# A fixed TensorE order for the first group of a state-space mixer

## The chip, the cores and the metric

The kernel runs on one core of one Trainium2 chip. The metric is the device time in microseconds (us) of one execution; the median of three runs before the change is 1351.42 us. TensorE (PE in the profile) multiplies, PEld is its loading of weights, VectorE is DVE, ScalarE is ACT, GpSimd is POOL, and SyncE (SP) starts most DMA transfers.

## The reference

The computation is a decoder trunk of two layers on 512 tokens of width 1024, in float32: a Mamba-2 mixer, a convolutional feed-forward block, differential attention, and a second feed-forward block. The change is in the mixer alone. Cut to what matters:

```python
zxbcdt = rms_norm(x, ln_g) @ in_w            # z | x, B, C | dt
xbc = silu(causal_dwconv(xbc, conv_w, conv_b))
dt = softplus(dt + dt_bias);  a = dt * (-exp(a_log))
# four groups of eight heads, four chunks of 128 tokens:
cb        = einsum('bclgn,bcsgn->bcgls', cc, bc)
y_diag    = einsum('bcgls,bgrcls,bcsgrp->bclgrp', cb, exp(segsum(a)), x*dt)
states    = einsum('bclgn,bgrcl,bclgrp->bcgrpn', bc, exp(a_cs[-1] - a_cs), x*dt)
# states are carried from chunk to chunk: S = S * exp(total of a) + states
y_off     = einsum('bclgn,bcgrpn,bgrcl->bclgrp', cc, states_in, exp(a_cs))
y = (y_diag + y_off + x * d_skip) * silu(z)
x = x + (rms_norm(y, per group) * norm_g) @ out_w
```

## The kernel before

A product of two float32 matrices is made of three passes in a reduced type: each operand is split into a high and a low part, and `mm3` (L196 to L198) multiplies high by high, low by high and high by low. One `mm3` on a block of 128 weight columns and 512 tokens is three matmuls; I call it a triple. A block of in_w has eight triples, one per 128 rows. Every chunk of weights is loaded by SP into a raw tile, its high part is made by ACT (`high`, L147), its low part by DVE (`low`, L151). `chunk(key)` hands out the next chunk and prepares the one two places further on in a fixed list, so asking for z's third block of group 0 prepares the first block of group 1.

The mixer is a loop over four groups. In each, `conv_block` makes B (bT), C (cT) and four blocks of x (xs): eight triples, then a convolution of three DVE steps and a SiLU on ACT. Then come four blocks of z, multiplied by the same input, with the scan of the group's four chunks between them. For chunk 0 to 3, called a, b, c and d in the code, the scan's steps are these:

- `fetch`: POOL starts the load of a row of sums, broadcast to all partitions, into m (128 x 8 x 128), and for chunks 1 to 3 of er. Tiles m have four buffers, er two.
- `decays`: POOL masks m (`affine_select`, L632), ACT takes eight exponentials (L637).
- `turned`: TensorE transposes B's chunk, ACT copies it (bt, L665).
- `masked`: TensorE multiplies C by B (cb, two instructions, L643), DVE multiplies m by it (L644).
- `tokens`: four transposes of xs (L652), then DVE makes xd (L654) and xe (L657).
- `states`: TensorE multiplies xe by bt (st, L682); for chunk 0 ACT copies the result to S (L685), for the others DVE scales the old S (L687) and adds (L688).
- `preceding`: for chunks 1 to 3, the previous S times C (yo, L673), then DVE multiplies er by it (L675).
- `products`: sixteen small matmuls xd by m (y, L696). `outputs`: DVE adds y, the skip term and er to xs (L705, L708).

ACT holds one table of functions at a time; the profile shows a load of a table (ACT_TABLE_LOAD) where SiLU and exponentials follow each other.

What sets the order: a planner simulates the program and gives each engine a list of instructions, by readiness in its own simulation and by place in the program. The engines then work through their lists in order, and an instruction whose input is late holds those behind it. `manual_schedule` for TensorE keeps the block's TensorE instructions in the order of the program. `issue_after(i)` queues what its block adds on i's engine behind i, without a wait for i to end.

Groups 1 to 3 use `woven` (L767): TensorE's order is fixed, and a table `at` says after which of z's 32 triples (`z_steps`, L731, counted from 0) which steps of the scan follow. In group 1 the table is read five triples later. Group 0 uses `weave` (L470) on `scan` (L750) and `z_blocks` (L722), and the planner orders TensorE too. In all groups the decays of chunks 0 and 1 stand in the program ahead of the third and fourth x block. The accumulator banks of the scan's steps come from a pool of four.

Of the kernel before, what the change touches and what calls it, by code (L numbers as in the profile page):

```python
# [18 lines left out]
P = 128  # L19
T = 512  # L20
D = 1024
KB = D // P
NT = T // P
# [16 lines left out]
def trunk_kernel(ctx: ExitStack, tc, x, ssm_ln_g, ssm_in_w, ssm_conv_w, ssm_conv_b, ssm_dt_bias,  # L40
# [4 lines left out]
    act, dve, pool, pe, sync = nc.scalar, nc.vector, nc.gpsimd, nc.tensor, nc.sync  # L45
# [192 lines left out]
    with tc.tile_pool(name="ph0", bufs=1) as p0:  # L238
# [24 lines left out]
        ps = aux_bank("pst")  # L263
# [117 lines left out]
        ps = aux_bank("pst")  # L381
# [134 lines left out]
    with tc.tile_pool(name="ssm_y", bufs=1) as yp, tc.tile_pool(name="ssm", bufs=1) as sp:  # L516
        def in_block(key):
            wh, wl = chunk(key)
            if key in ("in32", "in36"):
                return ps_b0 if key == "in32" else ps_b1  # L520
            ps = mm_bank("ps_" + key)
            for k in range(KB):
                state["last"] = mm3(ps, wh[:, k, :], wl[:, k, :], xgh[k], xgl[k], k == 0, k == KB - 1)
            return ps
# [16 lines left out]
        rr = [bp.tile([P, T], F32, tag="nr", name="nr_x")]  # L541
# [4 lines left out]
        ps = aux_bank("ps_dtt")  # L546
        with tc.issue_after(b1_end.ins):
            for c in range(NT):
# [12 lines left out]
                          in1=dtb.unsqueeze(1).to_broadcast([P, NT, NH]), op=ALU.add)  # L561
# [7 lines left out]
        for n in (13, 11, 9, 7, 5, 3):  # L569
# [21 lines left out]
        ncum = sp.tile([P, P], F32, name="ncum")  # L591
# [3 lines left out]
        ps = aux_bank("ps_cum")  # L595
# [10 lines left out]
        class Chunk:  # L606
# [22 lines left out]
            def decays(self):  # L629


                pool.affine_select(out=self.m, in_=self.m, pattern=[[0, HPG], [1, P]], compare_op=ALU.is_ge,  # L632
                                   fill=NEG, base=0, channel_multiplier=-1)
                for h in range(HPG):
                    v = self.m[:, 4 * (h % 2) + h // 2, :]
                    col = self.hh.start + h
                    act.activation(v, v, AF.Exp, bias=ncum[:, col:col + 1])  # L637

            def masked(self):

# [36 lines left out]
            def states(self):  # L677

                tag, c = self.tag, self.c
                if c < NT - 1:  # L680
                    ps = aux_bank("st" + tag)
                    pe.matmul(ps, self.bt, fl(self.xe), start=True, stop=True)  # L682
                    self.S = sp.tile([P, HPG, 64], F32, tag="S", name="S" + tag, bufs=2)
                    if c == 0:
                        act.activation(fl(self.S), ps, AF.Copy)  # L685
                    else:
                        dve.tensor_tensor(out=self.S, in0=self.prev.S, in1=self.per_head(et), op=ALU.mult)  # L687
                        dve.tensor_tensor(out=self.S, in0=byh(ps), in1=self.S, op=ALU.add)  # L688
# [30 lines left out]
                    add_to_stream(m, ps, 16, norm)  # L719
                    yield  # L720

        def z_blocks(g, zs):  # L722
            for b in range(4):
                ps = in_block("in%d" % (4 * g + b))
                z = sp.tile([P, T], F32, tag="z", name="z%d_%d" % (g, b), bufs=4)
                dve.tensor_tensor(out=z, in0=ps, in1=rr[0], op=ALU.mult)
                act.activation(z, z, AF.Silu)
                zs.append(z)
                yield

        def z_steps(g, zs):  # L731
            for b in range(4):
                wh, wl = chunk("in%d" % (4 * g + b))
                ps = mm_bank("ps_in%d" % (4 * g + b))
                for k in range(KB):
                    state["last"] = mm3(ps, wh[:, k, :], wl[:, k, :], xgh[k], xgl[k], k == 0, k == KB - 1)
                    if k == KB - 1:
                        z = sp.tile([P, T], F32, tag="z", name="z%d_%d" % (g, b), bufs=4)
                        dve.tensor_tensor(out=z, in0=ps, in1=rr[0], op=ALU.mult)
                        act.activation(z, z, AF.Silu)  # L740
                        zs.append(z)
                    yield

        def chunks(g, bT, cT, xs):
# [5 lines left out]
        def scan(cs):  # L750
            for t in range(NT + 1):
                if t < NT:
                    cs[t].tokens()
                    if t < NT - 1:
                        cs[t].turned()
                    cs[t].masked()
                if t == 0:
                    cs[2].decays()
                    cs[3].decays()
                if t:  # L760
                    cs[t - 1].preceding()
                    cs[t - 1].states()
                    cs[t - 1].products()
                    cs[t - 1].outputs()
                yield

        def woven(cs, g, zs):  # L767

            def pair(a, b):
                a.products()  # L770
                b.products()
                a.outputs()
                b.outputs()

            a, b, c, d = cs
            at = {0: (a.turned, b.turned, c.decays), 1: (a.masked, b.masked, d.decays),
                  10: (a.tokens,), 11: (b.tokens,), 13: (a.states,), 15: (b.preceding, b.states),
                  16: (lambda: pair(a, b), c.turned, c.masked), 18: (c.tokens,), 19: (c.preceding, d.tokens),
                  20: (d.masked,), 21: (c.states,), 24: (d.preceding,), 25: (lambda: pair(c, d),)}
            with tc.manual_schedule(engines={mybir.EngineType.PE}):  # L780
                behind = 5 if g == 1 else 0
                for n, _ in enumerate(z_steps(g, zs)):
                    for f in at.get(n - behind, ()):
                        f()

# [17 lines left out]
        for g in range(NG):  # L803
            bT = sp.tile([P, T], F32, tag="bT", name="bT%d" % g, bufs=2)
            cT = sp.tile([P, T], F32, tag="cT", name="cT%d" % g, bufs=2)
            xs_ = sp.tile([P, 4, T], F32, tag="xs", name="xs%d" % g, bufs=2)
            cs = chunks(g, bT, cT, xs_)
            for c in cs:
                c.fetch()
            conv_block(16 + g, "in%d" % (32 + g), bT)  # L810
            if g:
                prev = normed(*todo)
            conv_block(20 + g, "in%d" % (36 + g), cT)
            if g == 0:
                params_a()
            xs = [xs_[:, b, :] for b in range(4)]
            for b in range(4):
                if b >= 2:
                    cs[b - 2].decays()
                conv_block(4 * g + b, "in%d" % (16 + 4 * g + b), xs[b])  # L820
            zs = []
            if g:
                woven(cs, g, zs)
            else:
                weave(scan(cs), z_blocks(g, zs), 2, 3)
            acc = None
            for b in range(4):
                dve.tensor_tensor(out=xs[b], in0=xs[b], in1=zs[b], op=ALU.mult)
                sq = sp.tile([P, T], F32, tag="gsq", name="gsq%d_%d" % (g, b), bufs=2)
                act.activation(sq, xs[b], AF.Square)  # L830
                if b == 0:
                    acc = sq
                else:
                    a2 = sp.tile([P, T], F32, tag="gacc", name="gacc%d_%d" % (g, b), bufs=2)
                    (pool if b == 1 else dve).tensor_tensor(out=a2, in0=acc, in1=sq, op=ALU.add)
                    acc = a2
            factor = lambda: token_rsqrt(acc, sp, "g%d" % g, 512)
            if g == 0:
                params_b()
                todo = g, xs, factor()  # L840
            elif g < NG - 1:
                run(out_proj(g - 1, *prev, None))
                todo = g, xs, factor()
            else:
                op = out_proj(g - 1, *prev, None)
                for _ in range(3):
                    next(op)
                rt = factor()
                for _ in range(2):
                    next(op)  # L850
                prev = normed(g, xs, rt)
                run(op)
# [460 lines left out]
```

## Time and profile before

| | |
|---|---|
| Runs | 1350.94, 1351.42, 1352.56 us |
| Profiled execution | 1352.13 us |
| its span, first to last instruction | 1350.4 us |
| TensorE busy | 1342.4 us |
| DVE, ACT, POOL busy | 915.0, 646.2, 106.3 us |
| Group 0's x blocks, z and scan, on TensorE | from 27 to about 89 us of the span |
| Group 1's z and scan | about 122 to 158 us |
| Group 2's z and scan | about 213 to 247 us |

A row of a timeline has the start and the length in us, the engine, the line, the operation, what it writes and reads, shapes, how many in a row, and in brackets how long its engine sat idle before and what ended that. A row of stretches has the stretch and its length, then for each engine the busy us and the number of instructions, then TensorE's granted clock, the share of DMA time and GB/s. A row of waits has who waited, for whom, us in total, times, and the longest. The busy time of TensorE contains modelled ends: a matmul of 512 columns is shown as 0.39 us long while the next one starts earlier, so the distance of two starts tells more than the length.

### The profile page before, as it was taken

What the parts mean: (1) busy time and instruction counts of PE and PEld (TensorE: products, weight loads), DVE (VectorE), ACT (ScalarE), POOL (GpSimd) and SP (SyncE); (2) the same over time, 40 slices, a digit from 0 to 9 for tenths busy, and PEclk for the clock granted to TensorE, in tenths of its full rate; (3) what the DMA queues carried; (4) which work ended last, traced back from release to release, by engine and by line L of the source; (5) the groups of instructions that cost most, each with busy time, mean ns of one, the idle gap of its engine ahead of it and who ended that gap; (6) DMA issues with size and microseconds to landing.
All of it is one profiled execution on the core that took longest, in us unless ns stands there. A gap on an engine that the chain in (4) does not pass through costs nothing.

```text
span 1350.4 us, 16886 instructions
## 1 busy us (share of the span) xinstructions
PE 1342.4 (99%) x6423; PEld 1097.3 (81%) x6423; DVE 915.0 (68%) x1525; ACT 646.2 (48%) x1060; POOL 106.3 (8%) x142
## 2 busy tenths in 40 slices
PE   9999999999999999999999999999999999999998
PEld 7878788888888888888888887777888888888887
DVE  4989888788877774267754556778777773367743
ACT  5696553742444442234433556777654442134430
POOL 6230400200110000000001200000110000000000
PEclk9999999999999999999999999999999999999999
DMA  7453433432333333333323422221232332333322
GB/s 204 143 166 90 138 109 110 133 94 71 94 94 94 94 98 105 94 94 94 100 80 102 133 78 89 69 86 36 76 92 87 103 94 94 94 104 99 94 94 78
DMA packets 179825, 134.98 MB, mean 100 GB/s; under 512 B 6492, under 2 KB 163552, under 8 KB 179744
## 3 DMA queue, kind: packets, MB, share of 16 engines
q1 hardware_dynamic: 173872, 120.73, 29.7%
q0 software_dynamic: 4592, 12.08, 2.8%
q10 hardware_dynamic: 1280, 1.10, 0.2%
q8 instruction: 50, 0.82, 0.2%
q14 instruction: 31, 0.25, 0.1%
HBM read 131.64 MB, written 2.25 MB: 99 GB/s over the span
## 4 chain that ended last, share of the span: by engine, by line
PE 93%; DVE 3%; ACT 2%; issue 1%; DMA 0%; POOL 0%; SPq 0%; ACTq 0%; DVEq 0%
PE ps_g L197 6%; PE ps_g L198 6%; PE ps_g L196 6%; PE ps_u L198 6%; PE ps_u L196 6%; PE ps_u L197 6%; PE ps_in L196 4%; PE ps_in L197 4%; PE ps_in L198 4%; PE ps_d L198 3%; PE ps_d L196 3%; PE ps_d L197 3%; PE ps_d L915 3%; PE ps_d L914 3%; PE ps_d L913 3%; PE ps_o L197 2%
## 5 line engine op out<-in xcount | busy, mean ns | idle before, releaser
L196 PE MATMUL ps_u<-xgh,wh_u 128*128 128x512 f32 x352 | 137.6, 391 | 0.0
L197 PE MATMUL ps_g<-xgl,wh_g 128*128 128x512 f32 x352 | 137.2, 390 | 0.0
L196 PE MATMUL ps_g<-xgh,wh_g 128*128 128x512 f32 x352 | 137.2, 390 | 0.0
L198 PE MATMUL ps_u<-xgh,wl_u 128*128 128x512 f32 x352 | 137.2, 390 | 0.0
L198 PE MATMUL ps_g<-xgh,wl_g 128*128 128x512 f32 x352 | 137.2, 390 | 0.0
L197 PE MATMUL ps_u<-xgl,wh_u 128*128 128x512 f32 x352 | 137.1, 390 | 0.0
L196 PE MATMUL ps_in<-xgh,wh_in 128*128 128x512 f32 x304 | 126.4, 416 | 0.0
L151 DVE TENSOR_TENSOR wl_d<-wr_d,wh_d 128x1024 fp32r<-128x1024 f32 (+1 forms) x46 | 54.2, 1179 | 96.9 <-ACT wh_d L147 96.7
L197 PE MATMUL ps_in<-xgl,wh_in 128*128 128x512 f32 x304 | 119.5, 393 | 0.0
L198 PE MATMUL ps_in<-xgh,wl_in 128*128 128x512 f32 x304 | 119.4, 393 | 0.0
L147 ACT ACTIVATE wh_d<-wr_d 128x1024 fp32r<-128x1024 f32 (+1 forms) x46 | 47.1, 1024 | 130.6 <-PE ps_d L915 62.4
L874 DVE TENSOR_TENSOR uu<-ps_u,nr_f 128x512 f32<-128x512 f32 x44 | 30.4, 692 | 78.0 <-PE ps_u L198 77.9
L940 ACT ACTIVATE hh<-vg 128x512 fp32r<-128x512 f32 x44 | 27.8, 632 | 114.9 <-DVE vg L939 114.9
L197 PEld LDWEIGHTS ps_g<-xgl,wh_g 128*128 128x128 f32 x352 | 66.1, 188 | 13.9 <-DVE xgl L413 0.3
L198 PEld LDWEIGHTS ps_g<-xgh,wl_g 128*128 128x128 f32 x352 | 66.1, 188 | 13.7
L198 PEld LDWEIGHTS ps_u<-xgh,wl_u 128*128 128x128 f32 x352 | 66.1, 188 | 13.7
L197 PEld LDWEIGHTS ps_u<-xgl,wh_u 128*128 128x128 f32 x352 | 66.2, 188 | 13.6
L196 PEld LDWEIGHTS ps_g<-xgh,wh_g 128*128 128x128 f32 x352 | 66.1, 188 | 13.6
L196 PEld LDWEIGHTS ps_u<-xgh,wh_u 128*128 128x128 f32 x352 | 66.1, 188 | 13.5
L147 ACT ACTIVATE wh_g<-wr_g 128x1024 fp32r<-128x1024 f32 x44 | 46.7, 1062 | 51.6 <-PE ps_u L197 32.3
L198 PE MATMUL ps_d<-hh,wl_d 128*128 128x512 f32 x176 | 68.6, 390 | 0.0
L196 PE MATMUL ps_d<-hh,wh_d 128*128 128x512 f32 x176 | 68.6, 390 | 0.0
(359 smaller groups left out, 3180.5 us busy)
## 6 DMA issues: line engine op xcount, KB each, us to landing
wr_g<-in_ffn_up_w_dram SPq DMA_DIRECT2D x44, 512.0 KB, 3.7
wr_u<-in_ffn_up_w_dram SPq DMA_DIRECT2D x44, 512.0 KB, 3.7
wr_d<-in_ffn_down_w_dram SPq DMA_DIRECT2D x42, 512.0 KB, 3.6
wr_in<-in_ssm_in_w_dram SPq DMA_DIRECT2D x40, 512.0 KB, 3.8
m<-cumd POOLq DMA_DIRECT2D x16, 512.0 KB, 5.0
wr_out<-in_ssm_out_w_dram SPq DMA_DIRECT2D x16, 512.0 KB, 3.3
wr_k<-in_kv_w_dram SPq DMA_DIRECT2D x8, 512.0 KB, 3.7
wr_q<-in_q_w_dram SPq DMA_DIRECT2D x8, 512.0 KB, 3.6
```

The costliest lines, as they stand in the source:

```text
L147: return act.activation(self.wh[:, :self.n], self.raw[:, :self.n], AF.Copy)
L151: return eng.tensor_tensor(out=self.wl[:, :self.n], in0=self.raw[:, :self.n], in1=self.wh[:, :self.n].bitcast(F32), op=ALU.subtract)
L196: pe.matmul(ps, wh, xh, start=start, stop=False)
L197: pe.matmul(ps, wh, xl, start=False, stop=False)
L198: return pe.matmul(ps, wl, xh, start=False, stop=stop).ins
L874: dve.tensor_tensor(out=u, in0=ps, in1=r, op=ALU.mult)
L913: pe.matmul(pss[b], hh[k][:, ts], wh[:, k - k0, :], start=k == 0, stop=False)
L914: pe.matmul(pss[b], hh[k][:, ts], wl[:, k - k0, :], start=False, stop=False)
L915: pe.matmul(pss[b], hl[k][:, ts], wh[:, k - k0, :], start=False, stop=k == stop)
L940: act.activation(h, ga, AF.Copy)
```

## The change

Group 0 is woven as the others are, with a table of its own. The decays of its four chunks stand together after the eighth triple of z. The SiLU of z's second block is queued on ACT behind the last exponential of chunk 3, and what is prepared when z's third block is asked for (the high part of group 1's first block) behind the last exponential of chunk 1. The copy of the first state goes to DVE. In group 1 the states of chunks 0 and 2 come one triple later; groups 2 and 3 keep their table.

```diff
             def decays(self):
...
-                    act.activation(v, v, AF.Exp, bias=ncum[:, col:col + 1])
+                    self.decayed = act.activation(v, v, AF.Exp, bias=ncum[:, col:col + 1]).ins
...
-                    if c == 0:
+                    if c == 0 and self.g == 0:
+                        dve.tensor_copy(fl(self.S), ps)
+                    elif c == 0:
                         act.activation(fl(self.S), ps, AF.Copy)
...
-        def z_steps(g, zs):
+        def z_steps(g, zs, cs):
             for b in range(4):
-                wh, wl = chunk("in%d" % (4 * g + b))
+                if g == 0 and b == 2:
+                    with tc.issue_after(cs[1].decayed):
+                        wh, wl = chunk("in%d" % b)
+                else:
+                    wh, wl = chunk("in%d" % (4 * g + b))
...
-                        act.activation(z, z, AF.Silu)
+                        if g == 0 and b == 1:
+                            with tc.issue_after(cs[3].decayed):
+                                act.activation(z, z, AF.Silu)
+                        else:
+                            act.activation(z, z, AF.Silu)
...
             a, b, c, d = cs
-            at = {0: (a.turned, b.turned, c.decays), 1: (a.masked, b.masked, d.decays),
-                  10: (a.tokens,), 11: (b.tokens,), 13: (a.states,), 15: (b.preceding, b.states),
-                  16: (lambda: pair(a, b), c.turned, c.masked), 18: (c.tokens,), 19: (c.preceding, d.tokens),
-                  20: (d.masked,), 21: (c.states,), 24: (d.preceding,), 25: (lambda: pair(c, d),)}
+            both = lambda: pair(a, b)
+            rest = lambda: pair(c, d)
+            if g == 0:
+                at = {0: (a.turned, b.turned), 7: (a.decays, b.decays, c.decays, d.decays),
+                      11: (a.tokens,), 12: (b.tokens,), 14: (a.states,), 16: (a.masked, b.masked),
+                      17: (b.preceding, b.states), 20: (both, c.turned, c.masked), 22: (c.tokens,),
+                      23: (c.preceding, d.tokens), 24: (d.masked,), 26: (c.states,), 28: (d.preceding,),
+                      29: (rest,)}
+            else:
+                at = {0: (a.turned, b.turned, c.decays), 1: (a.masked, b.masked, d.decays),
+                      10: (a.tokens,), 11: (b.tokens,), 13: (a.states,), 15: (b.preceding, b.states),
+                      16: (both, c.turned, c.masked), 18: (c.tokens,), 19: (c.preceding, d.tokens),
+                      20: (d.masked,), 21: (c.states,), 24: (d.preceding,), 25: (rest,)}
+            if g == 1:
+                at[14], at[22] = at.pop(13), at.pop(21)
...
             for b in range(4):
-                if b >= 2:
+                if g and b >= 2:
                     cs[b - 2].decays()
...
-            if g:
-                woven(cs, g, zs)
-            else:
-                weave(scan(cs), z_blocks(g, zs), 2, 3)
+            woven(cs, g, zs)
```

More of the change, by code (lines that the diff above doesn't have):

```diff
@@ L720, in out_proj @@
                     yield
-        def z_blocks(g, zs):
+        def z_steps(g, zs, cs):
             for b in range(4):
[L724 to L729, printed above, removed]
-        def z_steps(g, zs):
-            for b in range(4):
-                wh, wl = chunk("in%d" % (4 * g + b))
+                if g == 0 and b == 2:
[3 more added lines that the diff above has]
+                    wh, wl = chunk("in%d" % (4 * g + b))
                 ps = mm_bank("ps_in%d" % (4 * g + b))
@@ L739, in z_steps @@
                         dve.tensor_tensor(out=z, in0=ps, in1=rr[0], op=ALU.mult)
-                        act.activation(z, z, AF.Silu)
+                        if g == 0 and b == 1:
[3 more added lines that the diff above has]
+                            act.activation(z, z, AF.Silu)
                         zs.append(z)
@@ L748, in chunks @@
             return cs
[L750 to L765, printed above, removed]
         def woven(cs, g, zs):
@@ L775, in woven @@
             a, b, c, d = cs
-            at = {0: (a.turned, b.turned, c.decays), 1: (a.masked, b.masked, d.decays),
-                  10: (a.tokens,), 11: (b.tokens,), 13: (a.states,), 15: (b.preceding, b.states),
-                  16: (lambda: pair(a, b), c.turned, c.masked), 18: (c.tokens,), 19: (c.preceding, d.tokens),
-                  20: (d.masked,), 21: (c.states,), 24: (d.preceding,), 25: (lambda: pair(c, d),)}
+            both = lambda: pair(a, b)
[13 more added lines that the diff above has]
+                at[14], at[22] = at.pop(13), at.pop(21)
             with tc.manual_schedule(engines={mybir.EngineType.PE}):
                 behind = 5 if g == 1 else 0
-                for n, _ in enumerate(z_steps(g, zs)):
+                for n, _ in enumerate(z_steps(g, zs, cs)):
                     for f in at.get(n - behind, ()):
```

## The prediction

> **What bounds the kernel now.** I read the page first (busy shares and the chain that ended last), then TensorE's waits, then stretches of the state-space stage, and last the engines' timelines inside them.
>
> ```profile
> span 1350.4 us, 16886 instructions
> PE 1342.4 (99%) x6423; PEld 1097.3 (81%) x6423; DVE 915.0 (68%) x1525; ACT 646.2 (48%) x1060; POOL 106.3 (8%) x142
> PE 93%; DVE 3%; ACT 2%; issue 1%; DMA 0%; POOL 0%; SPq 0%; ACTq 0%; DVEq 0%
> ```
>
> TensorE (PE) is busy for all but 8.0 us of 1350.4 and is 93% of the chain. Every us of TensorE's own sequence counts, and nothing else counts unless TensorE waits for it. Its total waits are few:
>
> ```profile
> PE warm L262 <- DVE ones L202: 1.1, 1, 1.1
> PE st L682 <- DVE xe L657: 0.8, 2, 0.6
> ```
>
> The first is the start of the program. The second is group 1's two state matmuls, which the last part of the change touches. But "busy" hides delays, because a matmul's end is modelled: it lasts 0.39 us, while the next starts earlier. So I count starts. Nine steps lie between these two rows, 2.04 us, or 0.227 us for one 512-column matmul in a steady run:
>
> ```profile
> 50.12 0.39 PE L198 MATMUL ps_in<-xgh,wl_in 128*128 128x512 f32 x1
> 52.16 0.39 PE L198 MATMUL ps_in<-xgh,wl_in 128*128 128x512 f32 x1
> ```
>
> Now the three scans, each from about its first small matmul to the end of its last y: groups 0, 1 and 2. The first rows are the stretches with TensorE's matmuls of in_w (ps_in) counted, the last is group 1's matmuls of out_w in the same stretch.
>
> ```profile
> 52.57:88.60 36.03, 25.58 (x97) 17.57 (x97) 2.05 (x3) 1.00 0.60 188
> 125.82:157.64 31.82, 21.16 (x75) 13.39 (x75) 2.06 (x3) 1.00 0.35 112
> 213.56:242.93 29.37, 21.14 (x75) 13.38 (x75) 2.10 (x4) 1.00 0.34 99
> 125.82:157.64 31.82, 1.49 (x5) 0.94 (x5) 0.00 (x0) 1.00 0.35 112
> ```
>
> Take the big matmuls off at 0.227 us. Group 0 has 36.03 - 97 x 0.227 = 14.0 us left for its scan, group 1 has 31.82 - 80 x 0.227 = 13.7, group 2 has 29.37 - 75 x 0.227 = 12.3. The small matmuls of the scan are the same in each. So group 2, which has the fixed order and no wait named, shows what the fixed order costs when its inputs are ready, and the whole change can win at most 14.0 - 12.3 and 13.7 - 12.3.
>
> **The change, part by part.** *Group 0's order.* Its stretch also holds two bT transposes and one of cum that group 2's leaves out. At 0.11 us a step, with a change of shape or two, I estimate 0.5. Left to win: 1.7 - 0.5 = 1.2 us. The bounds of this part: 1.7 if none of the 0.5 is real, and a loss if a wait enters, so I follow TensorE to each place.
>
> ```profile
> 27.07:51.00 23.93, 22.45 (x97) 17.97 (x97) 3.42 (x5) 1.00 0.29 78
> 212.70 0.39 PE L196 MATMUL ps_in<-xgh,wh_in 128*128 128x512 f32 x1
> 220.90 0.60 PE L652 MATMUL xs<-ident,xs 128*128 128x128 f32 x4
> 223.88 1.02 PE L682 MATMUL st<-xe,bt 128*128 128x512 f32 x2
> 228.66 0.55 PE L696 MATMUL y<-m,xd 128*64 128x128 f32 x6
> 241.04 1.97 PE L696 MATMUL y<-m,xd 128*64 128x128 f32 x32
> ```
>
> The first row holds group 0's four x blocks, 4 x 24 matmuls and one hanging over the edge, so z starts at about 51.0. Group 2's z starts at 212.70. Group 0 gets the same steps as group 2, some triples (three matmuls, 0.68 us) later, with the cb matmuls (0.46, an estimate) moved behind the states. Two cum transposes and one of parameters come between, some 0.6. So group 0 reaches its first tokens at 51.0 + 8.2 + 0.68 - 0.46 + 0.6 = 60.0, its first state at 51.0 + 11.2 + 0.8 = 63.0, the products of chunks 0 and 1 at 51.0 + 16.0 + 4 x 0.68 + 0.6 = 70.3 (chunk 1's 1.0 later, at 71.3), those of chunks 2 and 3 12.4 us after, at 82.7. What each place needs:
>
> ```profile
> 60.28 1.58 POOL L632 TENSOR_SCALAR_AFFINE_SELECT m<-m 128x1024 f32<-128x1024 f32 x1
> 62.20 2.06 POOL L632 TENSOR_SCALAR_AFFINE_SELECT m<-m 128x1024 f32<-128x1024 f32 x1 [0.34 <-DMA m<-cumd]
> 68.33 1.09 POOL L632 TENSOR_SCALAR_AFFINE_SELECT m<-m 128x1024 f32<-128x1024 f32 x1 [2.51 <-DMA m<-cumd]
> 58.96 0.62 ACT L536 ACTIVATE xs<-ctmp 128x512 f32<-128x512 f32 x1
> 59.81 0.63 ACT L727 ACTIVATE z<-z 128x512 f32<-128x512 f32 x1 [0.23 <-DVE z L726]
> 64.32 0.60 ACT L685 ACTIVATE S<-st 128x512 f32<-128x512 f32 x1 [3.88 <-PE st L682]
> 64.81 1.05 ACT L147 ACTIVATE wh_in<-wr_in 128x1024 fp32r<-128x1024 f32 x1
> 66.99 0.63 ACT L727 ACTIVATE z<-z 128x512 f32<-128x512 f32 x1 [1.13 <-DVE z L726]
> 67.63 1.28 ACT L637 ACT_TABLE_LOAD   x1
> 68.92 9.47 ACT L637 ACTIVATE m<-m,ncum 128x128 f32<-128x128 f32 x32
> 60.83 1.28 DVE L654 TENSOR_TENSOR xd<-xs,dt 128x512 f32<-128x512 f32 x2
> 62.03 1.28 DVE L657 TENSOR_TENSOR xe<-xd,dec 128x512 f32<-128x512 f32 x2
> 73.82 1.22 DVE L644 TENSOR_TENSOR m<-m,cb 128x1024 f32<-128x1024 f32 x1 [1.12 <-ACT m L637]
> 72.85 1.09 PE L696 MATMUL y<-m,xd 128*64 128x128 f32 x16
> ```
>
> Tokens need xs, done at 59.58: 0.4 to spare. The first state needs xe, between 62.2 and 63.2 by the DVE's order of its 0.6 us steps: a wait of 0 to 0.3, I take 0.15. The products need m masked. POOL's queue keeps its order, m's loads and then the selects, whose first two end at 61.86 and 64.26. ACT is free from 60.44, since it then sits 3.88 us before the copy S, which now goes to VectorE. Table load to 61.7, eight exponentials at 9.47 / 32 = 0.296: chunk 0 done at 64.2, chunk 1 at 66.6. The cb matmuls come at about 65.5, so the masks (1.22 each) end at 67.1 and 68.3, or near 71 if four VectorE steps of 0.69 (S, z, er, the new S) get in between. That is 0 to 0.7 of wait at 70.3, and I take 0.2, nearer the free end, because VectorE has waits of its own here. Chunk 3: select ends 69.42, exponentials 71.8, ten us before 82.7. Sum for group 0: -1.2 + 0.15 + 0.2 = -0.85.
>
> *Edits hidden by the above.* z's second SiLU and the split of the next group's first block (L147 at 64.81) move behind the exponentials, to 67 to 73. That block is multiplied after the 96 of z, at about 86, with VectorE's low part (1.2) before it; uncovered, the wait would be the lateness itself. Its load on SP is not tied. Behind ACT's pinned steps queue the next chunk's bt copy, needed some 4 us ahead of 82.7 (an estimate from group 2's steps), and the remaining SiLUs, needed after the stage. The S copy costs VectorE 0.69 where ACT took 0.60; yo comes three triples, 2 us, after the state. POOL's er load for chunk 3 and group 1's m loads stay behind the outputs and products that free their tiles, which come earlier or within 2 us of before.
>
> *Group 1's states.* Here a stall goes, so I ask what is late next.
>
> ```profile
> 135.91 0.40 PE L198 MATMUL ps_in<-xgh,wl_in 128*128 128x512 f32 x1
> 135.70 0.68 DVE L657 TENSOR_TENSOR xe<-xd,dec 128x512 f32<-128x512 f32 x1
> 136.53 1.10 PE L682 MATMUL st<-xe,bt 128*128 128x512 f32 x2 [0.23 <-DVE xe L657]
> 137.66 0.60 ACT L685 ACTIVATE S<-st 128x512 f32<-128x512 f32 x1 [2.95 <-PE st L682]
> 138.62 0.54 PEld L673 LDWEIGHTS yo<-cT,S 128*128 128x128 f32 x3
> 149.00 1.68 DVE L657 TENSOR_TENSOR xe<-xd,dec 128x512 f32<-128x512 f32 x1
> 150.82 1.10 PE L682 MATMUL st<-xe,bt 128*128 128x512 f32 x2 [0.56 <-DVE xe L657]
> 152.93 0.68 DVE L688 TENSOR_TENSOR S<-st,S 128x512 f32<-128x512 f32 x1
> 153.84 0.54 PEld L673 LDWEIGHTS yo<-cT,S 128*128 128x128 f32 x3
> ```
>
> Chunk 0: the state could have started at 135.91 + 0.23 = 136.14 and waited 0.39. A triple later it starts at 136.14 + 0.69 = 136.83 without a wait. Its copy starts 1.13 after it and takes 0.60, so it ends at 138.56, and yo, now one triple behind it instead of two, loads at 138.60 against 138.62: nothing is won, the wait moves to yo. Chunk 2: the state still starts near 150.8, right behind xe, and the 0.56 before it is filled (0.7 by starts, an estimate). But yo needs the new S, which VectorE ends at 153.61, and yo loaded at 153.84. So 0.1 is won, or up to 0.7 if VectorE adds S ahead of its mask; at most 1.4, the whole excess over group 2. I take -0.2, near the row of S.
>
> **Sum:** -0.85 - 0.2 = -1.05 us. The profiled execution took 1352.13 us (1.73 around its span) and would take 1351.1; it stood 0.7 over the median of the runs, so 1351.42 becomes **1350.4**.
>
> **Rivals.** *Slower: the products wait.* Before, the planner was free to put z's matmuls ahead of the first y (72.85); now the rest of z queues behind the products at 70.3. If the order that the planner gives ACT and VectorE leaves the exponentials where they were (at 66.99 z's second SiLU went first, though chunks 0 and 1 stood ahead of it in the program), chunk 1's mask ends at 73.82 + 1.22 = 75.04. TensorE then waits 75.1 - 71.3 = 3.8, and -1.2 - 0.2 + 3.8 = +2.4: 1353.8. It decides from a mask end of about 72.7 on. For it: that earlier order. Against it: POOL's rows and ACT's 3.88 idle us.
>
> In the rows above, the granted clock, the third column from the end, is 1.00 in every stretch, waits of 0.6 us among them; no run here has a much longer wait in mid-kernel. The Trainium skill's page "TensorE: Matmul & The Clock Gate", in Part 1 on the HAM clock gate, says the clock falls to half after an idle window of about 3.4 us. By that rule this rival would cost an estimated 1.7 us more, about 1355.5.
>
> *Both stages reach group 2's figure:* -1.2 - 1.4 = -2.6, 1348.8. For it: groups 1 and 2 run the same order. Against it: the yo arithmetic.
>
> *Nothing is won:* waits of 0.3 at the state, 0.7 at the products, and some 0.1 at tokens take group 0's 1.2. 1351.4. For it: margins of 0.4 us at two places.
>
> **How the numbers follow.** Forecast 0.50, products wait 0.20, both reach group 2 0.17, nothing won 0.13. A change of 0.2%, 2.7 us, is about what a measurement of this kernel can tell from none. The forecast and "nothing" lie within. The best case ends at that border, so I count 0.10 of it and 0.02 of the forecast's edge as faster. The waiting case starts near it and grows with each further wait, so 0.18 is slower. The range reaches from the best case, with the runs' scatter (1350.94 to 1352.56) in mind, to 0.8 over the waiting case: 1348.6 to 1354.6.
>
> **What would show it.** Right: group 0's scan with about 13 us left beside its big matmuls; exponentials from about 62 in one block; no wait over 0.3 before y; group 1's wait at the states gone and its yo no earlier. Wrong: a TensorE wait released by VectorE's m at group 0's y, exponentials behind 67, weights of the next group late near 86, or group 1 at group 2's figure.

## The result, and the profile after

The changed kernel takes 1354.74 us (median of 14 runs, 1353.33 to 1356.39) against 1351.74 (14 runs, 1350.94 to 1352.56). The ratio is 1.0025, 95% interval 1.0018 to 1.0032: 3.0 us slower, where 1.0 us faster was forecast, and just above the range. The profiled execution took 1355.38 us. Its page shows the span, the busy time and the shares of the chain that ended last:

```profile
span 1353.7 us, 16886 instructions
PE 1344.4 (99%) x6423; PEld 1098.6 (81%) x6423; DVE 916.1 (68%) x1526; ACT 646.5 (48%) x1059; POOL 107.2 (8%) x142
PE 92%; DVE 4%; ACT 1%; issue 1%; POOL 1%; DMA 0%; SPq 0%; DVEq 0%; ACTq 0%; POOLq 0%
```

TensorE idles 9.3 us instead of 8.0 and is shown busy for 2.0 us more, though its 6423 instructions are as many as before. The waits of TensorE between 59 and 260 us (who waited, for whom, us in total, times, longest) name the idle part:

```profile
PE tr_g L445 <- DVE gacc L827: 2.0, 1, 2.0
PE y L698 <- DVE m L644: 0.7, 1, 0.7
PE yo L673 <- DVE S L690: 0.3, 1, 0.3
```

The wait at group 1's states (0.8 before) is gone in this trace. The largest wait is new, and it lies behind the stage that was changed: tr_g is the transposes of group 0's sum of squares (`token_rsqrt`, L445), for the norm between the scan and out_w. The sum is made in `gsq`, `gacc` (L822, L827): ACT squares four blocks, POOL adds the first two, VectorE the others.

First the scan itself, in TensorE's timeline from 59 to 90 us (its big matmuls left out), with the stretch that answers to the first of the prediction's three (97 matmuls of in_w in 35.88 us, in 36.03 before):

```profile
60.25 0.60 PE L652 MATMUL xs<-ident,xs 128*128 128x128 f32 x4
...
63.23 1.02 PE L682 MATMUL st<-xe,bt 128*128 128x512 f32 x2
...
71.26 2.22 PE L698 MATMUL y<-m,xd 128*64 128x128 f32 x32 [0.65 <-DVE m L644]
...
84.70 1.16 PE L673 MATMUL yo<-cT,S 128*128 128x128 f32 x8 [0.28 <-DVE S L690]
86.48 1.97 PE L698 MATMUL y<-m,xd 128*64 128x128 f32 x32
```

```profile
52.57:88.45 35.88, 26.11 (x97) 17.30 (x97) 2.06 (x3) 1.00 0.62 187
```

Left beside the big matmuls are 35.88 - 97 x 0.227 = 13.9 us; 14.0 stood there before, about 13 was forecast. The two groups of 32 y differ by 2.22 - 1.97 = 0.25 us, so the first group waited once more inside. ACT's and then VectorE's timelines show why the masks came late:

```profile
60.28 1.28 ACT L637 ACT_TABLE_LOAD   x1
61.72 7.14 ACT L637 ACTIVATE m<-m,ncum 128x128 f32<-128x128 f32 x24 [0.16 <-POOL m L632]
69.09 2.45 ACT L637 ACTIVATE m<-m,ncum 128x128 f32<-128x128 f32 x8 [0.23 <-POOL m L632]
71.56 1.28 ACT L739 ACT_TABLE_LOAD   x1
72.85 0.63 ACT L739 ACTIVATE z<-z 128x512 f32<-128x512 f32 x1
```

```profile
67.70 0.69 DVE L675 TENSOR_TENSOR er<-yo,er 128x512 f32<-128x512 f32 x1 [0.87 <-PE yo L673]
68.56 0.69 DVE L690 TENSOR_TENSOR S<-st,S 128x512 f32<-128x512 f32 x1 [0.17 <-PE st L682]
69.29 0.69 DVE L689 TENSOR_TENSOR S<-S,dec 128x512 f32<-128x512 f32 x1
69.90 2.34 DVE L644 TENSOR_TENSOR m<-m,cb 128x1024 f32<-128x1024 f32 x2
```

The exponentials were ready: chunk 1's ended at about 61.72 + 16 x 0.297 = 66.5, and cb was there soon after 65.5. But VectorE's list has three steps of er and S ahead of the masks, and the first of them waits 0.87 us for yo.

Now behind the stage, the same work before and after. Before, in the timelines of POOL, VectorE and TensorE:

```profile
94.85 1.09 POOL L632 TENSOR_SCALAR_AFFINE_SELECT m<-m 128x1024 f32<-128x1024 f32 x1 [2.48 <-DMA m<-cumd]
96.20 1.96 POOL L835 TENSOR_TENSOR gacc<-gsq,gsq 128x512 f32<-128x512 f32 x1 [0.27 <-ACT gsq L830]
...
100.07 0.68 DVE L835 TENSOR_TENSOR gacc<-gacc,gsq 128x512 f32<-128x512 f32 x1
...
100.81 0.66 PE L445 MATMUL tr_g<-ident,gacc 128*128 128x128 f32 x4 [0.16 <-DVE gacc L835]
```

After, in the timelines of POOL, ACT, VectorE and TensorE:

```profile
88.13 0.56 POOL L622 DMA_DIRECT2D m<-cumd  x1 [8.04 <-PE y L698]
...
92.91 5.20 POOL L632 TENSOR_SCALAR_AFFINE_SELECT m<-m 128x1024 f32<-128x1024 f32 x2
98.08 1.28 POOL L827 TENSOR_TENSOR gacc<-gsq,gsq 128x512 f32<-128x512 f32 x1
...
99.39 1.15 ACT L822 ACTIVATE gsq<-xs 128x512 f32<-128x512 f32 x2 [1.83 <-POOL gacc L827]
...
100.05 1.49 DVE L827 TENSOR_TENSOR gacc<-gacc,gsq 128x512 f32<-128x512 f32 x2 [2.90 <-ACT gsq L822]
...
101.59 0.66 PE L445 MATMUL tr_g<-ident,gacc 128*128 128x128 f32 x4 [2.04 <-DVE gacc L827]
```

The products of chunks 2 and 3 now come as a pair, so they release their two m tiles together, at 88.13. Group 1's last two loads of m, the er loads and the last two selects follow on POOL's queue, and the selects, which took 1.09 us each before, take 5.20 for the two (3.17 and 2.07, one by one). POOL's first addition stands behind them and starts 1.9 us later than before, though its input (ACT's first two squares) was ready at 95.85. Most of that is the selects' length: the later m load takes 6.4 us to land, at 95.4, so with a select of 1.09 behind it the addition could have started near 96.5, an estimate, 0.3 us later than before.

This queue could be seen in the trace of before, behind group 1's scan, which ran in the fixed order already and whose products came as a pair. POOL's timeline there:

```profile
162.18 4.22 POOL L632 TENSOR_SCALAR_AFFINE_SELECT m<-m 128x1024 f32<-128x1024 f32 x2
166.37 2.25 POOL L835 TENSOR_TENSOR gacc<-gsq,gsq 128x512 f32<-128x512 f32 x1
```

TensorE has no wait at the tr_g behind that one. In group 0 of the change it does: ACT has two tiles for the squares and must wait for POOL's addition, so the sum ends at 101.54 instead of 100.75. And TensorE arrives sooner: 241 matmuls of in_w stand ahead of tr_g in the trace, 249 before, since the planner, which orders TensorE again from here on, put it at another place. These 8 are 1.8 us. The later sum and the earlier place meet in a wait of 2.04 us. Of the 1.9 us by which it grew, 0.8 is the later sum and 1.1 the earlier arrival (the 1.8 of the place less 0.7 by which TensorE runs late).

Then comes what the span loses beyond the wait. TensorE's timeline behind tr_g, and the stretches (granted clock in the third column from the end):

```profile
102.55 0.56 PE L196 MATMUL ps_in<-xgh,wh_in 128*128 128x512 f32 x1
...
106.19 0.39 PE L196 MATMUL ps_in<-xgh,wh_in 128*128 128x512 f32 x1
```

```profile
102.00:104.00 2.00, 2.00 (x9) 1.63 (x8) 2.00 (x8) 2.00 (x9) 0.00 (x0) 0.66 0.00 0
104.00:106.00 2.00, 2.00 (x6) 1.52 (x6) 2.00 (x8) 1.98 (x5) 0.00 (x0) 0.50 0.01 4
106.00:108.00 2.00, 2.00 (x10) 1.66 (x9) 1.46 (x6) 1.61 (x3) 0.00 (x0) 0.99 0.05 7
```

Nine steps lie between those two rows, 3.64 us instead of 9 x 0.227 = 2.04: at the low clock 1.6 us are lost. It isn't so in every execution. The 14 times fall into two groups of seven, 1353.33 to 1354.20 and 1355.29 to 1356.39; the mean clock over the span is 0.999 in all of the longer group and in two of the shorter. A second trace of the same kernel (`e11_after_again`) belongs to the faster one.

### The profile page after: what moved, and what is told of

Read it like the earlier page. It is cut to its first block, busy times and chain, and to the rows that moved or that the text cites. A ratio compares the mean times of both kernels' runs of the same rounds, so it can differ in the third digit from the quotient of the medians.

```text
span 1353.7 us, 16886 instructions
## 1 busy us (share of the span) xinstructions
PE 1344.4 (99%) x6423; PEld 1098.6 (81%) x6423; DVE 916.1 (68%) x1526; ACT 646.5 (48%) x1059; POOL 107.2 (8%) x142
## 4 chain that ended last, share of the span: by engine, by line
PE 92%; DVE 4%; ACT 1%; issue 1%; POOL 1%; DMA 0%; SPq 0%; DVEq 0%; ACTq 0%; POOLq 0%
PE ps_g L197 6%; PE ps_g L196 6%; PE ps_g L198 6%; PE ps_u L196 6%; PE ps_u L197 6%; PE ps_u L198 6%; PE ps_in L196 5%; PE ps_in L197 5%; PE ps_in L198 5%; PE ps_d L196 3%; PE ps_d L197 3%; PE ps_d L198 3%; PE ps_d L905 3%; PE ps_d L907 3%; PE ps_d L906 3%; PE ps_o L198 2%
## 5 line engine op out<-in xcount | busy, mean ns | idle before, releaser
L197 PEld LDWEIGHTS ps_g<-xgl,wh_g 128*128 128x128 f32 x352 | 66.0, 188 | 13.9 <-DVE xgl L413 0.3
L196 PEld LDWEIGHTS ps_in<-xgh,wh_in 128*128 128x128 f32 x304 | 57.5, 189 | 13.6 <-issue 3.6
```

The costliest lines, as they stand in the source:

```text
L196: pe.matmul(ps, wh, xh, start=start, stop=False)
L197: pe.matmul(ps, wh, xl, start=False, stop=False)
```

## The experiments

I follow TensorE by its lag: the start of the same matmul of in_w in a trace, less its start in the first trace of the kernel before. "Ahead of tr_g" is the matmul at 98.44 us of that trace, "behind" the one at 124.28, ahead of group 1's scan, and "end" the one at 244.43, in group 2. Medians stand beside 1351.46 us of the kernel before for e1 to e4, 1351.45 for e5 to e8, and 1351.41 for e9 to e11.

| run | median us (runs) | ratio, 95% | ahead of tr_g | behind | end |
|---|---|---|---|---|---|
| after | 1354.74 (14) | 1.0025 (1.0018 to 1.0032) | +0.72 | +4.22 | +3.20 |
| e1_g1_only | 1351.33 (11) | 0.9999 (0.9990 to 1.0008) | +0.08 | -0.07 | -1.08 |
| e2_g0_only | 1355.25 (8) | 1.0025 (1.0015 to 1.0035) | +1.18 | +4.69 | +4.87 |
| e3_sum_on_dve | 1352.29 (11) | 1.0005 (0.9996 to 1.0013) | +1.05 | +1.16 | +0.14 |
| e4_tr_later | 1355.19 (11) | 1.0026 (1.0017 to 1.0035) | +0.82 | +2.80 | +2.59 |
| e5_products_later | 1352.13 (11) | 1.0004 (0.9995 to 1.0013) | -0.71 | +0.25 | -0.77 |
| e6_silu_free | 1354.43 (11) | 1.0020 (1.0011 to 1.0029) | +2.38 | +2.50 | +2.56 |
| e7_copy_on_act | 1352.37 (11) | 1.0005 (0.9996 to 1.0014) | +0.19 | +0.32 | -0.70 |
| e8_tr_earlier | 1359.19 (5) | 1.0053 (1.0041 to 1.0066) | +1.06 (at 93.00) | +7.95 | +6.93 |
| e9_before_again | 1351.20 (1) | | +0.37 | -0.05 | -0.84 |
| e10_tr_pinned | 1351.14 (11) | 0.9997 (0.9988 to 1.0006) | -0.64 | -1.06 | -0.89 |
| e11_after_again | 1354.01 (1) | | +0.17 | +2.06 | +1.82 |

A lag of one trace scatters: the kernel before, traced again (e9), lies 0.37 off ahead of tr_g and 0.84 at the end.

**e1_g1_only and e2_g0_only: which half costs?** Each is one part of the change alone. The first adds this to the kernel before; the second takes the same two lines from the changed kernel.

```diff
+            if g == 1:
+                at[14], at[22] = at.pop(13), at.pop(21)
```

> The kernel before, with group 1's states of chunks 0 and 2 one triple later and nothing else. Theory A (the whole loss lies in group 0 and the stretch behind it; group 1's part is a gain): TensorE's lag over the kernel before fell by 1.0 us across group 1's scan in the changed kernel, so 1350.7 here, 1.0 us under the kernel before. Rival B (that gain was only the other groups' lateness being absorbed, since VectorE and ScalarE had stood still for TensorE): no gain by itself, 1351.5 to 1351.9, and the wait at yo as worked out in the prediction.

> The changed kernel without group 1's part. Theory A: 1.0 us slower than the changed kernel, 1355.7, the waits at group 1's two state matmuls back (0.8 us in the profile) and the 2 us wait at group 0's tr_g still there. Rival B: as the changed kernel, 1354.7, since the late start of group 1 lets VectorE get ahead.

Group 0's part carries the loss: alone it gives the whole ratio of 1.0025, and its trace has the wait at tr_g (2.04 us), with a clock of 0.50 behind it. The waits at group 1's two states are back in that trace (1.0 us in all); the median, 0.5 us over the change's, lies between theory A and rival B and doesn't decide. Group 1's part alone is 0.1 us from nothing. Its first state wins nothing: the wait moved to the loading of yo, as the prediction worked out; in TensorE's weight loads of e1:

```profile
138.47 0.97 PEld L673 LDWEIGHTS yo<-cT,S 128*128 128x128 f32 x8 [0.42 <-ACT S L685]
```

Yet e1's trace gains 1.0 us across group 1's scan, which its runs don't show; e9 below takes that up.

**e3_sum_on_dve: is it POOL's late addition?** The changed kernel, with group 0's first addition on VectorE.

```diff
-                    (pool if b == 1 else dve).tensor_tensor(out=a2, in0=acc, in1=sq, op=ALU.add)
+                    (pool if b == 1 and g else dve).tensor_tensor(out=a2, in0=acc, in1=sq, op=ALU.add)
```

> The changed kernel with the first addition of group 0's squares (gacc) on VectorE instead of GpSimd, where it stood behind group 1's last two selects. Theory A (that queue makes group 0's sum late, TensorE waits 2.0 us at tr_g, and the lower granted clock that follows costs up to 1.7 more): the wait at tr_g falls under 0.5 us, the granted clock stays 1.00 behind it, and the time is 1351.7 (2.2 us of wait and, on average over the runs, about half of 1.7 us less). Rival C (the loss is made inside group 0's scan, by its waits at y and yo): under 0.5 us of change, 1354.3 to 1354.8.

In the main it is. VectorE's and TensorE's timelines of e3:

```profile
96.20 0.74 DVE L827 TENSOR_TENSOR gacc<-gsq,gsq 128x512 f32<-128x512 f32 x1 [0.15 <-ACT gsq L822]
...
98.90 1.48 DVE L827 TENSOR_TENSOR gacc<-gacc,gsq 128x512 f32<-128x512 f32 x2
```

```profile
100.43 0.66 PE L445 MATMUL tr_g<-ident,gacc 128*128 128x128 f32 x4 [0.32 <-DVE gacc L827]
```

The sum is there 1.2 us earlier, the wait is 0.32, the clock stays at 1.00, and 2.2 of the 3.0 us are gone. TensorE meets tr_g at nearly the same place (242 matmuls of in_w ahead of it), so at that place a sooner sum is enough. What stays, 0.8 us over the kernel before (within the interval of no change), would fit group 0's scan, which leaves TensorE 1.05 us late ahead of tr_g, but that isn't shown: at the end of the trace the lag is 0.14.

**e4_tr_later: or only the place in TensorE's list?** The changed kernel with the transposes behind the next x block. al_g, which takes their result to all tokens, follows later.

```diff
-            if g:
+            if g > 1:
                 prev = normed(*todo)
...
                 conv_block(4 * g + b, "in%d" % (16 + 4 * g + b), xs[b])
+                if g == 1 and b == 0:
+                    with tc.issue_after(state["last"]):
+                        rt = todo[2]()
+                    prev = normed(todo[0], todo[1], rt)
...
-                todo = g, xs, factor()
+                todo = g, xs, factor
```

> The changed kernel with group 0's four transposes of the sum (tr_g) queued on TensorE behind group 1's first x block, some 20 matmuls later, and what follows from them later too. Theory A: no wait at tr_g, granted clock 1.00, about 1351.5. Rival D (the sum is late for TensorE's later users too, and the wait comes back at al_g or at out_w's matmuls): the wait moves there, 1353 or more.

No wait at tr_g, but one of the same size at the next link; TensorE's timeline of e4:

```profile
104.71 0.60 PE L445 MATMUL tr_g<-ident,gacc 128*128 128x128 f32 x4
...
115.90 0.65 PE L455 MATMUL al_g<-ident,tr_g 128*128 128x128 f32 x4 [2.17 <-DVE tr_g L428]
```

The time is that of the changed kernel. Moving one link without the one that hangs on it moves the wait. No run tests the earlier place by itself: tr_g back behind 249 matmuls, with al_g moved as well and the addition left on POOL.

**e5_products_later: what is the fixed order of group 0 worth?** e3 with the masks, products and what follows one or two triples later.

```diff
-                      17: (b.preceding, b.states), 20: (both, c.turned, c.masked), 22: (c.tokens,),
-                      23: (c.preceding, d.tokens), 24: (d.masked,), 26: (c.states,), 28: (d.preceding,),
-                      29: (rest,)}
+                      17: (b.preceding, b.states), 22: (both, c.turned, c.masked), 23: (c.tokens,),
+                      24: (c.preceding, d.tokens), 25: (d.masked,), 27: (c.states,), 30: (d.preceding,),
+                      31: (rest,)}
```

> The changed kernel with the sum on VectorE, as in the run of that name, and group 0's products of chunks 0 and 1 after z's triple 22 instead of 20, what follows one or two triples later (products of chunks 2 and 3 after 31). Theory A (the two waits inside group 0's scan, 0.8 us and more at y and 0.25 at yo, are lateness of VectorE's masks and of its new S against a fixed place): the wait at y under 0.2 us, TensorE's lag at the end of the scan -0.2 instead of +0.9 us, and 1351.2. Rival E (VectorE's order moves along with the places, so the waits stay): no change, 1352.3.

The waits at y and yo are gone and TensorE leaves the stage 0.71 us ahead of the kernel before, 1.8 ahead of e3. But it loses the lead at once; TensorE's timeline of e5:

```profile
100.28 0.63 PE L445 MATMUL tr_g<-ident,gacc 128*128 128x128 f32 x4 [1.03 <-DVE s2t L398]
```

The sum ends at 100.14, only 0.2 us sooner than in e3, so an earlier TensorE waits longer (the row names s2t, VectorE's next step behind the sum), and the time is e3's. Theory A had the waits right and the time, 1351.2, wrong.

**e6_silu_free and e7_copy_on_act: do the other moves matter?** Both are e3 with one part undone: the SiLU of z's second block without its tie, and the copy of the first state back on ACT.

```diff
-                        if g == 0 and b == 1:
-                            with tc.issue_after(cs[3].decayed):
-                                act.activation(z, z, AF.Silu)
-                        else:
-                            act.activation(z, z, AF.Silu)
+                        act.activation(z, z, AF.Silu)
```

> The changed kernel with the sum on VectorE, and z's second SiLU free of its tie to the exponentials (the planner then puts it ahead of them). Theory A (exponentials as late as before hold up the products, as the prediction's slower rival has it): table load near 67, chunk 1's mask done near 74.6 instead of 72.3, the wait at y 2.4 us longer, so 1354.7 against 1352.3 with the tie. Rival F (the masks are late by VectorE's order anyway, the exponentials do not bind): under 0.7 us more, 1352.3 to 1353.0.

```diff
-                    if c == 0 and self.g == 0:
-                        dve.tensor_copy(fl(self.S), ps)
-                    elif c == 0:
+                    if c == 0:
```

> The changed kernel with the sum on VectorE, and the copy of group 0's first S back on ScalarE, where it stands ahead of the exponentials. Theory A: the table load waits for the copy, to about 64.9 instead of 60.3, exponentials of chunk 1 end near 70.5 instead of 66.7, its mask near 72.5 to 73, so 0.3 to 1.0 us more than 1352.3. Rival F (VectorE's order binds): no change.

Without the tie the SiLU goes first, and the slower rival of the prediction is there in kind. ACT's timeline of e6, then TensorE's:

```profile
65.73 0.63 ACT L737 ACTIVATE z<-z 128x512 f32<-128x512 f32 x1 [5.41 <-DVE z L736]
66.37 1.28 ACT L637 ACT_TABLE_LOAD   x1
67.67 7.71 ACT L637 ACTIVATE m<-m,ncum 128x128 f32<-128x128 f32 x26
```

```profile
71.59 1.09 PE L698 MATMUL y<-m,xd 128*64 128x128 f32 x16 [0.96 <-DVE m L644]
...
73.93 1.09 PE L698 MATMUL y<-m,xd 128*64 128x128 f32 x16 [1.24 <-DVE m L644]
```

It costs 2.1 us against e3 (1354.43 less 1352.29). The copy is free either way: on ACT it puts the exponentials off by 4.4 us, to 66.12, and in e7 the products come when they did in the change, because VectorE's list and not the exponentials decides.

```profile
66.12 9.18 ACT L637 ACTIVATE m<-m,ncum 128x128 f32<-128x128 f32 x31
```

```profile
71.18 2.08 PE L696 MATMUL y<-m,xd 128*64 128x128 f32 x28 [0.65 <-DVE m L644]
```

**e8_tr_earlier: what does such a wait cost?** The changed kernel with 13 more matmuls of in_w queued behind tr_g, so that TensorE arrives earlier and stands longer.

```diff
-            pe.transpose(ps[:, b * P:(b + 1) * P], acc[:, b * P:(b + 1) * P], ident)
+            state["tr"] = pe.transpose(ps[:, b * P:(b + 1) * P], acc[:, b * P:(b + 1) * P], ident).ins
...
             for k in range(KB):
+                if key in ("in20", "in21", "in22", "in23") or key == "in37" and k >= 4:
+                    with tc.issue_after(state["tr"]):
+                        state["last"] = mm3(ps, wh[:, k, :], wl[:, k, :], xgh[k], xgl[k], k == 0, k == KB - 1)
+                    continue
```

> The changed kernel with group 0's transposes of the sum (tr_g) put 13 big matmuls earlier on TensorE, so that their wait is about 2.9 us longer (some 5 us in all). Theory A (a wait costs its length, and a lower granted clock behind it as well, which follows a wait of 2 us in some runs and a wait of 5 us in all): 1354.7 + 2.9 + 0.8, about 1358.4, with all runs in one cluster and a granted clock under 1.00 behind the wait. Rival G (the lower clock has nothing to do with the wait): 1357.6, the clock low in about half of the runs as before.

TensorE's timeline of e8 and one of its stretches:

```profile
101.90 1.11 PE L445 MATMUL tr_g<-ident,gacc 128*128 128x128 f32 x4 [4.96 <-DVE gacc L831]
```

```profile
102.00:104.00 2.00, 2.00 (x7) 1.81 (x8) 1.72 (x6) 1.62 (x7) 0.00 (x0) 0.50 0.00 0
```

The wait grew by 2.9 us, the time over the kernel before by 4.7 (7.7 against 3.0), more than the 3.7 of theory A and the 2.9 of rival G. The clock is low for longer than in the first trace of the change: the four stretches of 2 us from 98 to 106 show 0.75, 0.50, 0.50 and 0.55, so the fall begins within the wait. The mean clock over the span is 0.997 in all five runs (0.999 or 1.000 in the runs of the change): here every execution pays for the clock, there, by the two groups of times, about half.

**e9_before_again and e11_after_again: what of a trace is luck?** Both are the two kernels as they were, traced once more.

> The kernel before, unchanged, traced a second time. The first trace had one subtraction xe of group 1 stretched to 1.68 us (0.68 elsewhere) while GpSimd's select started at the same moment, and TensorE waited 0.56 us for it. Theory H (that meeting is luck of one execution, so that single trace overstates what a later state can win): here xe takes 0.7 us and the wait at group 1's second state is under 0.3 us, the span 0.6 us shorter. Rival I (it is fixed by the order): xe at 1.6 to 1.7 us and the wait at 0.5 to 0.6 us again.

> The changed kernel, unchanged, traced a second time. Theory A: the wait of 2 us at group 0's tr_g is there again, whatever the time; if the granted clock falls behind it, the time lies at 1355.3 to 1356.4, if it stays at 1.00, at 1353.3 to 1354.2, so that the clock's share can be read off. Rival G (the two groups of times come from somewhere else): a time in the other group than the clock says.

In the first trace of before, group 1's xe of chunk 2 lasted 1.68 us and the state waited 0.56. In e9 it lasted 0.68 and the state didn't wait. POOL's select beside it, in the first trace of before and then xe and the select in e9:

```profile
149.02 1.10 POOL L632 TENSOR_SCALAR_AFFINE_SELECT m<-m 128x1024 f32<-128x1024 f32 x1
```

```profile
148.84 0.68 DVE L657 TENSOR_TENSOR xe<-xd,dec 128x512 f32<-128x512 f32 x1
...
149.06 1.41 POOL L632 TENSOR_SCALAR_AFFINE_SELECT m<-m 128x1024 f32<-128x1024 f32 x1 [0.22 <-DMA m<-cumd]
```

So the wait that group 1's part was to fill came and went with 0.2 us of POOL's timing. The kernel before gains 0.8 us across group 1's scan in e9 by this alone, so e1's gain of 1.0 in one trace is mostly luck. Nor does the part keep the wait away: in e11, which has it, xe took 1.68 again, and TensorE's timeline shows

```profile
152.64 1.10 PE L682 MATMUL st<-xe,bt 128*128 128x512 f32 x2 [0.54 <-DVE xe L657]
```

In e11 the clock was 1.00 from 98 to 108 us with the same wait of 2.04, and TensorE lost 2.06 - 0.17 = 1.9 us across tr_g, where the first trace of the change lost 4.22 - 0.72 = 3.5. The wait costs 1.9, the clock, where it falls, 1.6 more.

**e10_tr_pinned: a version with all links in place.** e5 with tr_g behind the first half of group 1's first x block and al_g's step behind its third.

```diff
+                if k == 3:
+                    state[key] = state["last"]
...
-            if g:
+            if g > 1:
                 prev = normed(*todo)
...
+                if g == 1 and b == 0:
+                    with tc.issue_after(state["in20"]):
+                        rt = todo[2]()
+                if g == 1 and b == 2:
+                    prev = normed(todo[0], todo[1], rt)
...
-                todo = g, xs, factor()
+                todo = g, xs, factor
```

> The kernel with products later and the sum on VectorE, with group 0's transposes of the sum (tr_g) tied behind the middle of group 1's first x block, some 18 places later on TensorE, and the transposes that spread the result (al_g) behind the end of its third x block, 49 places after them, so that VectorE's chain between the two, 9 to 11 us, fits. Theory A: no wait over 0.2 us from z of group 0 to the end of group 1's scan; TensorE's lag over the kernel before is -0.7 us behind group 0 and about -1.5 us behind group 1; 1350.6. Rival J (the later work of VectorE delays group 1's tokens or out_w's matmuls): a wait of 0.5 us or more there, 1351.3 or more.

TensorE has no wait from the z of group 0 to group 1's first state, and keeps the lead of the stage: 0.6 us ahead of tr_g, 1.1 behind it. Then it waits 0.31 and 0.42 us at group 1's states, against theory A, and its lead at the end, 0.89, is no more than that of the kernel before in e9 (0.84). The runs say 1351.14 against 1351.41, ratio 0.9997, where theory A had 1350.6. It is 3.3 us under the change, each against its own kernel before, and not to be told from the kernel before.

## Why the prediction was wrong

- **The step that failed** is the sentence that the outputs and products that free the tiles of POOL's er load and group 1's m loads "come earlier or within 2 us of before". It rests on the products of chunks 2 and 3 at 82.7. They came at 86.48, 3.8 later: about 0.3 us of lateness from ahead, 0.9 of waiting in the first products, 0.3 at the last yo, and 2.0 for three triples that stand ahead of that yo beside the two of the table (five, from 80.43 on). Measured, the last two m loads start at 88.13 and 88.99 (84.35 and 89.40 before), so one is 3.8 us later. The sentence also followed tiles to their loads and stopped there, and the sum has no term for what lies behind the stage. What mattered was the next in POOL's queue: two selects side by side, stretched to 5.20 us, and behind them the addition at 98.08 instead of 96.20. No sentence named tr_g as the first that waits behind the stage, though its wait of 0.16 in the trace of before said that it had no slack. The loss across tr_g is 1.9 to 3.5 us a trace; e3 takes away 2.2 us of the median.
- **The planner's new order** behind the stage (8 matmuls of in_w fewer ahead of tr_g) wasn't considered. By the trace it is the larger part of the growth of the wait (1.8 us of place, less 0.7 of lag, against 0.8 of sum); no run changed it alone. The edit is to group 0, but the order of all that follows comes out of the same simulation.
- **Arrivals** were right for the first half of the scan: tokens 60.25 (60.0 forecast), first state 63.23 (63.0), products 71.26 with 0.65 of waiting in it, so 70.6 (70.3). The first state's wait, 0.15 forecast, was nothing. The products of chunks 2 and 3 were 3.8 us late, as said.
- **The wait at the products**, a term of 0.2, was mis-sized: 0.65 + 0.25 = 0.9. The case "near 71, if four VectorE steps get in between" was named and priced too low; the second mask ended at 72.24. A wait of 0.28 at the last yo wasn't foreseen.
- **Group 0's order, -1.2**: with the waits taken out, e5 leaves the stage 0.7 us ahead, so this term was right in sign and 0.5 too large (one trace, with the products two triples later than in the change; e10, with the same scan, has 0.64). With them the change leaves it 0.2 to 0.7 late, in two traces.
- **The edits said to be hidden** inside the stage were: table load and SiLU at 71.56 and 72.85, no wait for weights, the copy of S free (e7).
- **Group 1, -0.2**: 0.1 by e1's runs, within their scatter, and the first state won nothing, by the arithmetic that was given. The stall at chunk 2 was priced from one trace, in which it happened to be there, and a later place doesn't fill it: with the part in, it is 0.54 us in e11 and 0.42 to 0.56 in e4, e6 and e10.
- **The slower rival** had the right side and, at 1353.8 or 1355.5, about the right time, by luck: the time was lost elsewhere and for another reason. Its mechanism is real (e6) and the tie on the SiLU prevents it.
- **The clock.** Behind the wait of 2.04 us the granted clock was 0.50 in one trace of the change and 1.00 in the other, 0.50 in e2's, and 1.00 behind e4's wait of 2.17; with 4.96 us it was 0.50. The Trainium skill's page "TensorE: Matmul & The Clock Gate", Part 1, gives an idle window of about 3.4 us that runs free of the kernel. The trace agrees that a long wait costs the clock, with e8's 4.96; that a wait of 2.04 can do so is not what its length says, and here the measurement decides. The rival's estimate of 1.7 us for it stands beside 1.6 measured.

What stays open: the shares of the later sum and of the earlier place in the loss; what decides which executions pay for the clock, which no run controls; and what makes POOL's selects long beside VectorE's work. The traces show where it happens. The select of 3.17 us runs beside VectorE's four products of xs and z, which take 2.50, in the change and behind group 1 in the kernel before; in e5, where the selects come apart and take 1.16 and 1.28, those four products take 3.39.

## What to carry to other kernels

Follow a change past the end of the stage that it touches, to the first instruction of the bounding engine that waits for anything, and along every queue that the stage shares (here POOL's): an engine with 8% load held the sum that TensorE needed next. Where that next wait already stands near zero in the profile, what the stage wins is waited away there, so move it first, and with it each link that hangs on it. If another part of the kernel runs the new order already, read the queues behind it too: here group 1's rows showed the long selects. Trace a kernel twice before pricing a stall of half a microsecond, and price a long wait of TensorE at its length plus the clock.

## What the hardware showed that I had not expected

- A wait of 2.04 us in mid-kernel can be followed by a granted clock of half for some 3.4 us, at 1.6 us: of the four traces with a wait of 2.04 to 2.17 us, two show it and two don't. The times of the change suggest about half of its executions; with 4.96 us it was all five. In e3 and e5, with waits of up to 1.03 us, the mean clock was 1.000 in all 22 runs.
- A VectorE step of 0.68 us (xe of group 1's chunk 2) takes 1.68 when POOL's select starts 0.02 us behind it (149.00 and 149.02 in the first trace of before) and stays at 0.68 when the select starts 0.22 behind (e9), where the select is the one that is longer, 1.41 for 1.10. In six of the 13 traces, with the select 0.02 or 0.03 us behind, it is xe that is long; in the other seven, with 0.03 to 0.22, it is the select (1.41 to 1.60).
